# All convolution gates ahead of the mamba gates, and layer norm, output projection and group norm among the last SSD group's steps

## The chip, the cores and the metric

The kernel runs on one core of a Trainium2 chip. The metric is the device time of one execution in microseconds (us). Engines are called as the profile calls them: PE (TensorE's matmuls), PEld (its weight loads), DVE (VectorE), ACT (ScalarE), POOL (GpSimd) and SP (the queue that issues most DMAs).

## The reference, cut to what matters

One layer of a hybrid decoder on 336 tokens (272 of a prompt with meta tokens, 8 sequences of 8 new ones). One input projection feeds a convolution branch (GLU, a depthwise convolution of width 31, layer norm, SiLU, output projection) and a Mamba-2 branch (short convolution, SSD, gated group norm, output projection). Two gates weigh the branches; a product-key expert mixer follows.

```python
proj = xn @ w_in + b_in
glu_in, z, xbc, dt_raw, gate_raw = split(proj)
ga, gb = split(glu_in)
u = ga * sigmoid(gb)
c = causal_depthwise(concat(conf_buf, u), conf_dw_w, conf_dw_b)
c = silu(layernorm(c, conf_ln_g, conf_ln_b))
y_a = c @ w_conf_out + b_conf_out
...
ys, h = ssd_segment(xs, dt, A, Bm, Cm, h, chunk)
y = gated_group_rmsnorm(ys + D_skip * xs, z, m_norm_w)
y_b = y @ w_m_out
g_a, g_b = split(sigmoid(gate_raw))
x = x + (g_a * y_a + g_b * y_b) @ w_o
x = x + peer(rmsnorm(x, norm2_w), peer_w_q, peer_keys, peer_u, peer_v)
```

## The kernel before

Features lie on the partitions, in tiles of 128 rows and 336 token columns (T); D_MODEL is 8 such tiles (KD). A projection to 128 features (`proj`) is 24 matmuls: for each of the eight input tiles the weight's high part times the input's high and low parts, then eight with the weight's low part. `weight` loads 128x1024 weights with a DMA on the SP queue into one of four `wraw` buffers, casts the high part `wh` on ACT and subtracts the low part `wl` on POOL, or now and then on DVE (the share `lm`); there are two `wh` and two `wl` buffers. `split` makes the same two parts of an input. PSUM has three banks for projections (`pj`), two for small products (`misc`) and two for the SSD's outputs (tag `y`).

The mixer's first part is a loop over 8 groups (G). In turn g, the generator `ssd` of group g gives its PE steps between the projections of group g+1 (`conf`, `xbc`, `zproj`), and the last steps of group g-1 (`old`) come in between too: `run(old, 1)` and `run(new, 1)` let one step of each go after each projection. The last step of a group squares its output on ACT, adds the two halves on POOL (tile `sq`) and sums groups on PE (`pgn`, line 641), then on DVE. In the last turn there is no next group: the projections of the gates (`gate`, 16 in all, `gates`) take that place, with the layer norm of the convolution branch written among them: `norm_mean` (PE sums `csum` and the last `cbuf` tile; ACT scales the mean; DVE subtracts it from eight `cbuf` tiles; ACT squares them into `sq`, of which there are four buffers), `norm_var` (PE sums eight squares), `norm_scale` (DVE scales `cbuf`, ACT applies SiLU).

After the groups: `gnorm_stats` (DVE and ACT make the group norm's factors from `pgn` into the tile `acs3`, which the profile calls acs), `gnorm` of each group (PE spreads the factors into `pgb`, DVE multiplies), `gsplit` (the parts `yh` on ACT and `yl` on POOL and DVE). `conf_out(j)` is the convolution branch's output projection of 128 features, from `ch` and `cl`, the two parts of `cbuf`, weighed with the gate. Then for each j the two projections of `w_mo` and the gated sum, its parts `mh` and `ml`, and the projections of `w_o`, `w_q` and the expert part.

The order: a scheduler orders each engine's instructions by the written order and its own estimates. From the SSD's first group on, and until `pin[0] = False`, PE's matmuls stand exactly in written order (`tc.keep_in_program_order` in `mm`). ACT's functions that need a table are chained in written order (`chain`). All engines execute in order.

Of the kernel before, what the change touches and what calls it, by code (L numbers as in the profile page):

```python
# [7 lines left out]
F32 = mybir.dt.float32  # L8
F32R = mybir.dt.float32r
# [4 lines left out]
OP = mybir.AluOpType  # L14
# [34 lines left out]
LM = (0.05, 0.05, 0.1, 0.5)  # L49
CE = 1  # L50
LOW = 400
NCO = 3
NW0 = 3
RB = 4
OH = 2
UV = 5
GLAG = 14
PLACE = (38, 50)
NB = 7
NG = 10  # L60
LASTP = 122
RIGHT = "right"
TOPK = 16
# [72 lines left out]
def body(tc, ia, oa, stop=None):  # L136
    nc = tc.nc
    with ExitStack() as top:
# [522 lines left out]

        def gsplit(g):
            yh = pair(F32R, "yh")
            yl = m2.tile([128, 2, T], F32R, name="yl", bufs=7) if g else pair(F32R, "yl")
            for b in range(2):
                split(yh[:, b, :], yl[:, b, :], ygf[g][:, b, :], on_pool=b == 0)
            yg.append((yh, yl))

        def gate_tile(j):
            if j < 6 or j > 11:  # L670
                return mp.tile([128, T], F32, name="gs", bufs=6)
            if j < 8:
                return tp.tile([128, T], F32, name="xnf", bufs=2)
            if j < 10:
                return tp.tile([128, MCAT], F32, name="mcat", bufs=2)[:, :T]
            if j == 10:
                idle.append(tp.tile([128, 2, T], F32, name="sz", bufs=2))
            return idle[0][:, j - 10]

        idle = []  # L680

        def gate(j):
            w = weight(ia["w_in"], 64 + j)
            p = pj()
            proj(p, w, xn)
            s = gate_tile(j)
            nc.scalar.activation(s, p, AF.Identity, bias=V("b_in", 64 + j))
            gates.append(s)

        gates, pv, squares, r24 = [], [], [], []  # L690

        def norm_mean():
            pm = pj()
# [4 lines left out]
            for k in range(KD):  # L698
                nc.vector.tensor_tensor(cb[:, k, :], cb[:, k, :], mu, op=OP.subtract)
                sq = tp.tile([128, T], F32, name="sq", bufs=4)  # L700
                nc.scalar.activation(sq, cb[:, k, :], AF.Square)
                squares.append(sq)

        def norm_var(ks):
            if not pv:
                pv.append(pj())
            for k in ks:
                mm(pv[0], ones, squares[k], start=(k == 0), stop=(k == KD - 1))

        def norm_scale():  # L710
            rs = tp.tile([128, T], F32, name="rs", bufs=2)
            rstd_of(rs, pv[0], D, tp)
            for k in range(KD):
                nc.vector.tensor_tensor(cb[:, k, :], cb[:, k, :], rs, op=OP.mult)
                act(cb[:, k, :], cb[:, k, :], AF.Silu, scale=V("ln_g", k), bias=V("ln_b", k))

        pgn = mp.tile([G, T], F32, name="pgn")
        csum = mp.tile([128, T], F32, name="csum")
# [13 lines left out]
        for g in range(G):  # L732
            new = ssd(g, *tiles, sz)
            if g + 1 < G:
                tiles, steps = xbc(g + 1)
                tasks = conf(g + 1) + steps
            else:
                lm[0] = LM[1]
                tasks = [lambda: gate(len(gates))] * 4
            run(old, 1)  # L740
            run(new, 1)
            for f in tasks:
                f()
                run(old, 1)
                run(new, 1)
            if g + 1 < G:
                sz, zsteps = zproj(g + 1)
                zsteps[0]()
# [1 line left out]
                zsteps[1]()  # L750
                old = new
            else:
                norm_mean()
                gate(4)
                run(new, 1)
                norm_var(range(4))
                run(new, 1)
                gate(5)
                run(new, 1)
                norm_var(range(4, KD))  # L760
                norm_scale()
                gate(6)
                run(new, 3)
        nc.scalar.dma_start(oa["mconv"], mnew)
        ls.close()

        m2 = mix.enter_context(tc.tile_pool(name="m2", bufs=1))
        r24.append(gnorm_stats())
        while len(gates) < NB:
            gate(len(gates))  # L770
        for g in range(G):
            gnorm(g, r24[0])
            if g % 3 == 1 and len(gates) < NG:
                gate(len(gates))
        pin[0] = False
        lm[0] = LM[2]
        ch = m2.tile([128, KD, T], F32R, name="ch")
        cl = m2.tile([128, KD, T], F32R, name="cl")
        for k in range(KD):
            split(ch[:, k, :], cl[:, k, :], cb[:, k, :])  # L780

        def conf_out(j):
            ga = gates[2 * j]
            act(ga, ga, AF.Sigmoid)
            w = weight(ia["w_co"], j)
            p = pj()
            proj(p, w, rows(ch, cl))
            nc.vector.scalar_tensor_tensor(ga, p, V("b_co", j), ga, op0=OP.add, op1=OP.mult)

        for j in range(NCO):  # L790
            conf_out(j)
        for g in range(G):
            gsplit(g)
        mh = m2.tile([128, KD, T], F32R, name="mh")
        ml = m2.tile([128, KD, T], F32R, name="ml")

        for j in range(KD):
            while len(gates) < min(2 * j + 3 + NG - 2 * NCO, 16):
                gate(len(gates))
            if j >= NCO:  # L800
                conf_out(j)
            ga, gb = gates[2 * j:2 * j + 2]
            act(gb, gb, AF.Sigmoid)
            p = pj()
            for s in range(2):
# [595 lines left out]
```

## Time and profile before

| what | us |
| --- | --- |
| median of 3 runs | 1430.98 (1429.24 to 1433.15) |
| the profiled execution's own time | 1431.76 |
| its span in the profile | 1430.0 |
| PE busy in the span | 1334.6 (93%) |
| DVE busy | 1007.1 (70%) |
| ACT busy | 525.8 (37%) |
| POOL busy | 582.3 (41%) |

The page also cuts the span into 40 slices of 35.75 us; a digit is the busy share of a slice in tenths, for PEclk the granted clock of TensorE:

```profile
PE   5899999999986999999999889999979999988997
PEclk9899999999987999999999999999989999999999
DMA  5444543544421444444999899999999999999993
```

The 12th and 13th slice (393 to 465 us) are the end of the SSD: PE 8 and 6 tenths, its clock 8 and 7 there. From the 20th slice on the expert part streams its tables, with DMA at 9 tenths. In the timelines a row is start, us, engine, line, operation, output<-inputs, shapes, count, and in brackets the engine's idle time ahead of it with what ended it. Rows of a group or a tile show the count, then ns of one: least, median, most.

### The profile page before, as it was taken

The numbers are of one execution on the slowest core, as the hardware profiler recorded it, in microseconds if no ns is written. First come the engines' busy times: TensorE is split into PE (matmuls) and PEld (weight loads), VectorE is DVE, ScalarE is ACT, GpSimd is POOL, SyncE is SP. The second block draws the span as 40 slices with busy tenths as digits, with TensorE's granted clock in tenths as the row PEclk, the third lists the DMA queues.
The fourth block names the chain that finished last, engine by engine and source line by source line (L and its number), as shares of the span: only waits on it lengthen the run. The fifth ranks groups of instructions, "written<-read, shape, count | busy, mean of one in ns | idle before, by whom it ended". The sixth has DMA issues, their size and how long they took to land.

```text
span 1430.0 us, 24506 instructions
## 1 busy us (share of the span) xinstructions
PE 1334.6 (93%) x9308; PEld 1261.6 (88%) x9308; DVE 1007.1 (70%) x2326; ACT 525.8 (37%) x1347; POOL 582.3 (41%) x483
## 2 busy tenths in 40 slices
PE   5899999999986999999999889999979999988997
PEld 3898888888865999989899889999979999987997
DVE  6787778777656312669999976787788787776423
ACT  4587776777646343443222221111111100111001
POOL 2267667767653666754221242222232222242100
PEclk9899999999987999999999999999989999999999
DMA  5444543544421444444999899999999999999993
GB/s 183 151 130 155 172 149 119 170 155 152 150 78 63 143 145 138 150 163 135 391 416 412 331 412 414 406 373 392 384 417 415 394 379 384 385 417 415 414 335 98
DMA packets 86806, 382.05 MB, mean 267 GB/s; under 512 B 10112, under 2 KB 15360, under 8 KB 66080
## 3 DMA queue, kind: packets, MB, share of 16 engines
q1 hardware_dynamic: 64144, 226.87, 44.1%
q0 software_dynamic: 20736, 151.00, 26.0%
q10 hardware_dynamic: 1808, 2.60, 0.5%
q8 instruction: 73, 1.20, 0.3%
q14 instruction: 45, 0.37, 0.1%
HBM read 367.41 MB, written 13.03 MB: 266 GB/s over the span
## 4 chain that ended last, share of the span: by engine, by line
PE 51%; DVE 13%; DMA 6%; ACT 1%; POOL 0%; issue 0%; DVEq 0%; ACTq 0%
PE va L1267 19%; PE pj L150 14%; PE pj L1176 12%; PE pg L1205 5%; DMA eraw<-in_vE_dram 3%; DVE ygat L1110 2%; DVE wuv L1102 2%; DMA eraw<-in_uT_dram 2%; DVE si L912 1%; DVE cand L955 1%; DMA nd<-x1d 1%; PE psc L1012 1%; DVE si L909 1%; DVE cand L949 1%; DVE cand L952 1%; DVE ci L909 0%
## 5 line engine op out<-in xcount | busy, mean ns | idle before, releaser
L990 POOL DMA_INDIRECT wuv<-in_peer_uv_dram,gid x144 | 179.7, 1248 | 511.2 <-DVE ygat L1110 218.5
L215 POOL TENSOR_TENSOR wl<-wraw,wh 128x1024 fp32r<-128x1024 f32 x115 | 274.9, 2390 | 190.1 <-ACT wh L214 107.3
L1176 PE MATMUL pj<-nd,eraw 128*128 128x176 f32 x2048 | 324.7, 318 | 10.5 <-DMA eraw<-in_uT_dram 7.2
L1267 PE MATMUL va<-S,eraw 128*128 128x176 f32 x2048 | 315.2, 314 | 11.0 <-DMA eraw<-in_vE_dram 11.0
L1176 PEld LDWEIGHTS pj<-nd,eraw 128*128 128x128 f32 x2048 | 311.5, 193 | 13.8 <-ACT S L1178 8.5
L1267 PEld LDWEIGHTS va<-S,eraw 128*128 128x128 f32 x2048 | 306.1, 191 | 15.7 <-DMA eraw<-in_vE_dram 13.9
L150 PE MATMUL pj<-ah,wh 128*128 128x336 f32 (+1 forms) x768 | 250.0, 334 | 2.4 <-ACT xnf L195 2.1
L150 PE MATMUL pj<-al,wh 128*128 128x336 f32 (+1 forms) x768 | 241.3, 322 | 0.0
L1110 DVE SCALAR_TENSOR_TENSOR ygat<-wuv,scg,ygat 128x1024 f32<-128x1024 f32 x128 | 163.9, 1280 | 53.4 <-ACT scg L1105 53.2
L214 ACT CAST wh<-wraw 128x1024 fp32r<-128x1024 f32 x128 | 134.4, 1050 | 148.9 <-PE pj L150 79.4
L1102 DVE SCALAR_TENSOR_TENSOR wuv<-wuv,x2m 128x1024 f32<-128x1024 f32 x128 | 155.9, 1218 | 38.2 <-DMA wuv<-in_peer_uv_dram,gid 38.2
L1104 ACT ACTIVATE scg<-scg 128x1 f32<-128x1 f32 x144 | 29.0, 202 | 401.9 <-DVE wuv L1102 401.7
L393 DVE SCALAR_TENSOR_TENSOR pcv<-ccat,vec,pcv 128x272 f32<-128x272 f32 x464 | 151.7, 388 | 17.9 <-ACT pcv L391 17.9
L150 PEld LDWEIGHTS pj<-ah,wh 128*128 128x128 f32 x768 | 148.5, 194 | 12.2 <-issue 4.4
L150 PEld LDWEIGHTS pj<-al,wh 128*128 128x128 f32 x768 | 148.7, 194 | 1.1 <-DVE al L215 0.5
L150 PE MATMUL pj<-ah,wl 128*128 128x336 f32 (+1 forms) x768 | 138.7, 320 | 0.0
L150 PEld LDWEIGHTS pj<-ah,wl 128*128 128x128 f32 x768 | 123.1, 190 | 0.8 <-issue 0.7
L1178 ACT ACTIVATE S<-pj 128x176 f32<-128x176 f32 x128 | 37.7, 311 | 155.4 <-PE pj L1176 155.3
L1205 PE MATMUL pg<-oh 128*128 128x64 bf16 x1056 | 76.3, 241 | 0.0
L1205 PEld LDWEIGHTS <-oh 128*128 128x128 bf16 x1056 | 71.6, 117 | 2.4
L1212 DVE TENSOR_TENSOR S<-S,pg 128x192 f32<-128x192 f32 (+1 forms) x66 | 31.7, 508 | 50.5 <-PE pg L1205 50.4
L408 DVE SCALAR_TENSOR_TENSOR pj<-mcat,vec,pj 128x360 f32<-128x360 f32 x96 | 56.4, 587 | 0.5 <-ACT pj L406 0.3
(343 smaller groups left out, 1691.5 us busy)
## 6 DMA issues: line engine op xcount, KB each, us to landing
eraw<-in_uT_dram SPq DMA_DIRECT2D x128, 512.0 KB, 11.5
eraw<-in_vE_dram SPq DMA_DIRECT2D x128, 512.0 KB, 10.0
wraw<-in_w_in_dram SPq DMA_DIRECT2D x80, 512.0 KB, 3.6
st<-in_state_dram SPq DMA_DIRECT2D x8, 1024.0 KB, 5.2
out_ssm_s_dram<-st SPq DMA_DIRECT2D x8, 1024.0 KB, 4.8
wraw<-in_w_mo_dram SPq DMA_DIRECT2D x16, 512.0 KB, 3.5
wraw<-in_w_q_dram SPq DMA_DIRECT2D x16, 512.0 KB, 3.6
wraw<-in_w_co_dram SPq DMA_DIRECT2D x8, 512.0 KB, 3.5
```

The source lines that it names most:

```text
L150: i_ = nc.tensor.matmul(*a_, **kw)
L214: (nc.vector.tensor_copy if on_dve else nc.scalar.copy)(h, src)
L215: (nc.gpsimd if on_pool else nc.vector).tensor_tensor(l, src, h.bitcast(F32), op=OP.subtract)
L393: t = nc.vector.scalar_tensor_tensor(o, i_, wv, a_, op0=OP.mult, op1=OP.add)
L408: nc.vector.scalar_tensor_tensor(o, cat[:, w:w + n], wv, o, op0=OP.mult, op1=OP.add)
L990: i_ = nc.gpsimd.indirect_dma_start(out=u, out_offset=None, in_=ia["peer_uv"], in_offset=bass.IndirectOffsetOnAxis(ap=gid[:, c:c + 1], axi ...
L1102: nc.vector.scalar_tensor_tensor(u[:, :D], u[:, :D], 1.0, x2m if c < NPICK else x2e, op0=OP.mult, op1=OP.mult, accum_out=w)
L1110: nc.vector.scalar_tensor_tensor(a_, u[:, D:], scg[:, c:c + 1], a_, op0=OP.mult, op1=OP.add)
L1176: i_ = nc.tensor.matmul(p[:, :ND], raw[:, k, :], nd[:, k, :], start=(k == 0), stop=(k == KD - 1))
L1178: nc.scalar.activation(Sv(b), p[:, :ND], AF.Gelu)
L1205: i_ = nc.tensor.matmul(pg[:, q, :], B[:, q // 4, :, q % 4], A[:, c_, q // 4, :, q % 4], start=(c_ == 0), stop=(c_ == 2))
L1267: i_ = nc.tensor.matmul(va[k // 2][:, k % 2], raw[:, k, :], Sv(b), start=False, stop=(b == 127), skip_group_check=True)
```

## The change

The gates are made in another order: all eight of the convolution branch (`j` even) first, then the eight of the mamba branch; in the list `gates` the first eight are the convolution's. The last turn of the group loop has seven gates as its tasks instead of four. `norm_mean` is written behind the first of them instead of behind the fourth, and adds its squares on POOL, so that `norm_scale`, which takes over the variance's matmul, needs one product instead of eight; it is written behind the fourth gate and makes `ch` and `cl` as well. The last three steps of the SSD have `conf_out` 0 to 2 between them, `gnorm_stats` is followed by a gate and `conf_out` 3 and 4, and `gnorm`, `gsplit` and `conf_out` 5 to 7 are written in one loop. Three gates follow; the last five stand one each ahead of the `w_mo` projections. `cl` takes idle tiles of other names (ccat, sz, mcat), some gates have new tiles (ge, gx).

```diff
...
@@ -661,33 +658,46 @@
 
         def gsplit(g):
             yh = pair(F32R, "yh")
-            yl = m2.tile([128, 2, T], F32R, name="yl", bufs=7) if g else pair(F32R, "yl")
+            yl = m2.tile([128, 2, T], F32R, name="yl", bufs=8)
             for b in range(2):
                 split(yh[:, b, :], yl[:, b, :], ygf[g][:, b, :], on_pool=b == 0)
             yg.append((yh, yl))
 
...
         idle = []
 
-        def gate(j):
+        def gate():
+            n = len(gates)
+            j = 2 * n if n < KD else 2 * (n - KD) + 1
             w = weight(ia["w_in"], 64 + j)
             p = pj()
             proj(p, w, xn)
-            s = gate_tile(j)
+            s = gate_tile(n)
             nc.scalar.activation(s, p, AF.Identity, bias=V("b_in", 64 + j))
             gates.append(s)
 
-        gates, pv, squares, r24 = [], [], [], []
+        ch = mp.tile([128, KD, T], F32R, name="ch")
+        cl = []
+
+        def conf_out(j):
+            ga = gates[j]
+            act(ga, ga, AF.Sigmoid)
+            w = weight(ia["w_co"], j)
+            p = pj()
+            proj(p, w, lambda k: (ch[:, k, :], cl[k]))
+            nc.vector.scalar_tensor_tensor(ga, p, V("b_co", j), ga, op0=OP.add, op1=OP.mult)
+
+        gates, squares, r24 = [], [], []
 
         def norm_mean():
             pm = pj()
@@ -699,20 +709,28 @@
                 nc.vector.tensor_tensor(cb[:, k, :], cb[:, k, :], mu, op=OP.subtract)
                 sq = tp.tile([128, T], F32, name="sq", bufs=4)
                 nc.scalar.activation(sq, cb[:, k, :], AF.Square)
-                squares.append(sq)
-
-        def norm_var(ks):
-            if not pv:
-                pv.append(pj())
-            for k in ks:
-                mm(pv[0], ones, squares[k], start=(k == 0), stop=(k == KD - 1))
+                if k:
+                    nc.gpsimd.tensor_tensor(squares[0], squares[0], sq, op=OP.add)
+                else:
+                    squares.append(sq)
 
         def norm_scale():
             rs = tp.tile([128, T], F32, name="rs", bufs=2)
-            rstd_of(rs, pv[0], D, tp)
+            p = pj()
+            mm(p, ones, squares[0], start=True, stop=True)
+            rstd_of(rs, p, D, tp)
             for k in range(KD):
                 nc.vector.tensor_tensor(cb[:, k, :], cb[:, k, :], rs, op=OP.mult)
                 act(cb[:, k, :], cb[:, k, :], AF.Silu, scale=V("ln_g", k), bias=V("ln_b", k))
+            for k in range(KD):
+                if k in (0, 1):
+                    cl.append(tp.tile([128, CCAT], F32R, name="ccat", bufs=2)[:, :T])
+                elif k in (2, 4):
+                    t = tp.tile([128, 2, T], F32R, name="sz", bufs=2) if k == 2 else pair(F32R, "cl")
+                    cl.extend(t[:, c_, :] for c_ in range(2))
+                elif k > 5:
+                    cl.append(tp.tile([128, MCAT], F32R, name="mcat", bufs=2)[:, :T])
+                split(ch[:, k, :], cl[k], cb[:, k, :])
 
         pgn = mp.tile([G, T], F32, name="pgn")
         csum = mp.tile([128, T], F32, name="csum")
@@ -736,13 +754,18 @@
                 tasks = conf(g + 1) + steps
             else:
                 lm[0] = LM[1]
-                tasks = [lambda: gate(len(gates))] * 4
+                tasks = [gate] * 7
             run(old, 1)
             run(new, 1)
-            for f in tasks:
+            for n, f in enumerate(tasks):
                 f()
                 run(old, 1)
                 run(new, 1)
+                if g + 1 == G:
+                    if n == 0:
+                        norm_mean()
+                    elif n == 3:
+                        norm_scale()
             if g + 1 < G:
                 sz, zsteps = zproj(g + 1)
                 zsteps[0]()
@@ -750,56 +773,33 @@
                 zsteps[1]()
                 old = new
             else:
-                norm_mean()
-                gate(4)
-                run(new, 1)
-                norm_var(range(4))
-                run(new, 1)
-                gate(5)
-                run(new, 1)
-                norm_var(range(4, KD))
-                norm_scale()
-                gate(6)
-                run(new, 3)
+                for j in range(3):
+                    conf_out(j)
+                    run(new, 1)
         nc.scalar.dma_start(oa["mconv"], mnew)
         ls.close()
 
         m2 = mix.enter_context(tc.tile_pool(name="m2", bufs=1))
         r24.append(gnorm_stats())
-        while len(gates) < NB:
-            gate(len(gates))
+        gate()
+        conf_out(3)
+        conf_out(4)
         for g in range(G):
             gnorm(g, r24[0])
-            if g % 3 == 1 and len(gates) < NG:
-                gate(len(gates))
+            gsplit(g)
+            if g % 2 and g < 6:
+                conf_out(5 + g // 2)
+        for _ in range(3):
+            gate()
         pin[0] = False
         lm[0] = LM[2]
-        ch = m2.tile([128, KD, T], F32R, name="ch")
-        cl = m2.tile([128, KD, T], F32R, name="cl")
-        for k in range(KD):
-            split(ch[:, k, :], cl[:, k, :], cb[:, k, :])
-
-        def conf_out(j):
-            ga = gates[2 * j]
-            act(ga, ga, AF.Sigmoid)
-            w = weight(ia["w_co"], j)
-            p = pj()
-            proj(p, w, rows(ch, cl))
-            nc.vector.scalar_tensor_tensor(ga, p, V("b_co", j), ga, op0=OP.add, op1=OP.mult)
-
-        for j in range(NCO):
-            conf_out(j)
-        for g in range(G):
-            gsplit(g)
         mh = m2.tile([128, KD, T], F32R, name="mh")
         ml = m2.tile([128, KD, T], F32R, name="ml")
 
         for j in range(KD):
-            while len(gates) < min(2 * j + 3 + NG - 2 * NCO, 16):
-                gate(len(gates))
-            if j >= NCO:
-                conf_out(j)
-            ga, gb = gates[2 * j:2 * j + 2]
+            if len(gates) < 2 * KD:
+                gate()
+            ga, gb = gates[j], gates[KD + j]
             act(gb, gb, AF.Sigmoid)
             p = pj()
             for s in range(2):
```

The constants NCO, NB and NG go; the rest of the cut is `gate_tile`, which picks a gate's tile. Line numbers of the changed kernel are 3 lower in the code ahead of line 660 (L215 becomes L212, L638 becomes L635).

The first place is POOL in the last group's first steps. `sq<-sq` of L638 adds the two halves of group 6's squares for `pgn`; `wx` are products of the last group. Before:

```order
L585 TENSOR_TENSOR xg<-xg,sz 128x336
L215 TENSOR_TENSOR wl<-wraw,wh 128x1024
L638 TENSOR_TENSOR sq<-sq 128x336
L215 TENSOR_TENSOR wl<-wraw,wh 128x1024
L533 TENSOR_TENSOR wx_4561<-xt_4558,wd_202 80x256
L215 TENSOR_TENSOR wl<-wraw,wh 128x1024
L533 TENSOR_TENSOR wx_4623<-xt_4620,wd_226 128x256
L533 TENSOR_TENSOR wx_4632<-xt_4629,wd_242 128x256
```

Now, with the layer norm's seven additions as L713:

```order
L582 TENSOR_TENSOR xg<-xg,sz 128x336
L212 TENSOR_TENSOR wl<-wraw,wh 128x1024 x2
L530 TENSOR_TENSOR wx_4562<-xt_4559,wd_202 80x256
L212 TENSOR_TENSOR wl<-wraw,wh 128x1024
L713 TENSOR_TENSOR sq<-sq 128x336 x7
L635 TENSOR_TENSOR sq<-sq 128x336
L530 TENSOR_TENSOR wx_4660<-xt_4657,wd_226 128x256
L530 TENSOR_TENSOR wx_4669<-xt_4666,wd_242 128x256
```

Group 6's addition moved behind two weight splits, the first `wx` and the seven new additions; the other two `wx` stand behind it as before.

The second place is PE at the first `pgb`, the spreading of the group norm's factors; `pj<-ah` is a gate's projection, `pst` the last state update, `pgn` the last group's sum. Before:

```order
L150 MATMUL pst_4960<-wx_4561,Bm 128x256
L150 MATMUL pst_4961<-wx_4561,Bm 128x256
L150 MATMUL pgn<-sq,cstm 8x336
L150 LDWEIGHTS id_256
L150 MATMUL pgb<-acs_4992,id_256 128x336
L150 LDWEIGHTS id_256
L150 MATMUL pgb<-acs_4992,id_256 128x336
L150 MATMUL pj<-ah,wh 128x336
```

Now, where `pj<-ch` is a projection of `conf_out` (the one ahead of these rows is `conf_out` 3; this is the end of `conf_out` 4):

```order
L147 MATMUL pj<-ch,wh 128x336
L147 MATMUL pj<-mcat,wh 128x336
L147 MATMUL pj<-ch,wl 128x336 x8
L147 LDWEIGHTS id_256
L147 MATMUL pgb<-acs_5114,id_256 128x336
L147 LDWEIGHTS id_256
L147 MATMUL pgb<-acs_5114,id_256 128x336
L147 MATMUL pj<-ch,wh 128x336
```

`pgn` no longer stands right ahead of the first `pgb`: a gate and `conf_out` 3 and 4, 72 matmuls, stand between them.

More of the change, by code (lines that the diff above doesn't have):

```diff
@@ L51 @@
 LOW = 400
-NCO = 3
 NW0 = 3
@@ L58 @@
 PLACE = (38, 50)
-NB = 7
-NG = 10
 LASTP = 122
@@ L667, in gsplit, with gate_tile @@
             yg.append((yh, yl))
-        def gate_tile(j):
-            if j < 6 or j > 11:
+        def gate_tile(n):
+            if n < 3 or 7 <= n < 10:
                 return mp.tile([128, T], F32, name="gs", bufs=6)
-            if j < 8:
+            if n < 5:
+                return mp.tile([128, T], F32, name="ge", bufs=2)
+            if n < 7:
                 return tp.tile([128, T], F32, name="xnf", bufs=2)
-            if j < 10:
-                return tp.tile([128, MCAT], F32, name="mcat", bufs=2)[:, :T]
-            if j == 10:
+            if n == 10:
                 idle.append(tp.tile([128, 2, T], F32, name="sz", bufs=2))
-            return idle[0][:, j - 10]
+            return idle[0][:, n - 10] if n < 12 else m2.tile([128, T], F32, name="gx", bufs=4)
         idle = []
-        def gate(j):
+        def gate():
+            n = len(gates)
+            j = 2 * n if n < KD else 2 * (n - KD) + 1
             w = weight(ia["w_in"], 64 + j)
```

## The prediction

> **What bounds the kernel now.** I read three views of the profile in this order: the busy time by stage, the waits of TensorE (PE), and the timelines of the engines in the stage that the change rewrites. The page's span, and the stages (start and end in us, length; busy us and instructions of PE, weight load, VectorE, ScalarE, GpSimd; PE's granted clock; DMA share; GB/s):
>
> ```profile
> span 1430.0 us, 24506 instructions
> 300.00:380.00 80.00, 78.34 (x549) 69.66 (x550) 66.18 (x182) 57.23 (x138) 57.49 (x57) 1.00 0.45 150
> 396.50:460.80 64.30, 42.92 (x233) 36.16 (x233) 41.34 (x74) 35.61 (x67) 26.32 (x22) 0.79 0.20 65
> 460.80:580.00 119.20, 119.20 (x777) 119.20 (x776) 35.69 (x44) 48.10 (x63) 69.65 (x31) 1.00 0.43 139
> ```
>
> PE is the bound: before 380 it is 98% busy, after 460.8 it has no gap. Between lie 64.3 us in which it idles 21.4 us and is granted 0.79 of its clock. That is the end of the SSD, and the change reorders just this. The rest of the program keeps its order, so what is won or lost here moves all that follows by as much. PE's waits in this stage (line, releaser, total us, times, longest):
>
> ```profile
> PE pgb L150 <- DVE acs L225: 12.0, 1, 12.0
> PE pst L150 <- DVE st L595: 5.0, 1, 5.0
> PE pst L150 <- DVE dec L543: 2.1, 1, 2.1
> PE pgb L150 <- DVE xg L660: 2.0, 2, 1.1
> PE pgn L150 <- DVE st L595: 0.3, 1, 0.3
> ```
>
> Together 21.4 us. PE runs its instructions in the order written here, so each wait stops all behind it. PE's timeline (start, us; in brackets the idle time before):
>
> ```profile
> 380.59 0.43 PE L150 MATMUL pj<-ah,wh 128*128 128x336 f32 x1
> 384.51 0.73 PE L150 MATMUL pgn<-sq,cstm 128*8 128x336 f32 x2
> 386.71 0.42 PE L150 MATMUL pj<-ah,wh 128*128 128x336 f32 x1
> 396.52 0.83 PE L150 MATMUL pj<-csum,cst 128*128 128x336 f32 x2
> 397.50 0.57 PE L150 MATMUL pj<-ah,wh 128*128 128x336 f32 x1
> 402.13 2.42 PE L150 MATMUL pj<-sq,cst 128*128 128x336 f32 x8
> 406.65 0.70 PE L150 MATMUL pst<-wx,xt 128*128 128x256 f32 x2 [2.10 <-DVE dec L543]
> 409.41 0.63 PE L150 MATMUL pj<-ah,wh 128*128 128x336 f32 x1
> 430.77 1.28 PE L150 MATMUL pgn<-sq,cstm 128*8 128x336 f32 x2 [0.28 <-DVE st L595]
> 444.01 0.72 PE L150 MATMUL pgb<-acs,id 96*128 96x336 bf16 x2 [11.96 <-DVE acs L225]
> 444.31 0.69 PE L150 MATMUL pj<-ah,wh 128*128 128x336 f32 x1
> 444.81 0.48 PE L150 MATMUL pj<-al,wh 128*128 128x336 f32 x1
> 450.17 0.46 PE L150 MATMUL pgb<-acs,id 96*128 96x336 bf16 x2
> 457.30 124.32 PE pj L150 x808
> ```
>
> The last row, of the chain of waits, gives the full pace: 124.32/808 = 0.154 us a matmul, 3.69 us for a projection of 24. The projection after the longest wait took 450.17 - 444.31 = 5.86 us: **a wait costs itself and a slow restart of about 2.2 us** (matmuls of 0.48 us).
>
> **The change, part by part.** Counts first: 16 gates, 8 projections of conf_out, 32 weight splits and their DMAs stay; they change places. PE does one matmul of the squares (2 rows) in place of eight (16 rows). GpSimd (POOL) gets seven additions.
>
> *Work removed.* Four squares took 2.42 us, eight 4.84, one keeps 0.6: **4.2 us** less on PE, all in this stage.
>
> *The 12.0 us.* From the last pgn to the first pgb passed 444.01 - 430.77 = 13.2 us, with no PE work between. Now gate 7, conf_out 3 and 4 stand there: 3 x 3.69, with pgn's 0.7 = 11.8. The chain loses the cl subtractions among its VectorE steps and gains one weight split ahead of it and one weight cast on ScalarE between its table loads; I take it as it was: a remainder of 1.4, less the 0.8 by which pgn (1.28 for 0.73) and pgb (0.72 for 0.46) were themselves slow then: **0.6** left, bounds 0 and 3.
>
> *The 5.0, 0.3 and 2.0 us.* The state update waited for VectorE, which was in the middle of eight scalings of cbuf. Now conf_out 1 (3.69) stands between the two updates, and the scalings are over by then. Between the pairs of pgb there are projections of 3.69 for VectorE's four products. I take 0 for all three.
>
> *A new wait at pgn of group 6.* This is the price. The mean and squares move to just after gate 0, and on ScalarE and POOL the square sum of group 6 now stands behind them, while on PE its matmul (pgn) still follows gate 1. Behind pgn queue the transposes and everything of the last group.
>
> ```profile
> 382.93 0.41 ACT L622 ACTIVATE Bm<-xt,cstm 64x128 f32<-64x128 f32 x1
> 383.43 1.05 ACT L214 CAST wh<-wraw 128x1024 fp32r<-128x1024 f32 x1
> 397.96 0.45 ACT L697 ACTIVATE rs<-pj 128x336 f32<-128x336 f32 x1 [1.63 <-PE pj L150]
> 400.52 0.48 ACT L701 ACTIVATE sq<-cbuf 128x336 f32<-128x336 f32 x1 [2.11 <-DVE cbuf L699]
> 384.72 2.36 POOL L215 TENSOR_TENSOR wl<-wraw,wh 128x1024 fp32r<-128x1024 f32 x1 [2.99 <-ACT wh L214]
> 419.11 0.92 POOL L638 TENSOR_TENSOR sq<-sq 128x336 f32<-128x336 f32 x1 [0.60 <-ACT sq L637]
> L699 DVE TENSOR_TENSOR cbuf<-cbuf,rs x8: 497/498/2651, 398.4 to 403.3; 128x336 f32<-128x336 f32 x8
> ```
>
> PE: mean matmuls 380.6 to 381.6 (396.52 to 397.50 before: 0.98), gate 1 to 385.3. ScalarE is free at 383.3 (after Bm): mean 383.8; first subtraction on VectorE, first square by 385.2; then the weight cast, 386.3. POOL's weight split, ahead of the additions, runs 386.4 to 388.8. Then seven additions and group 6's own, 8 x 0.92 = 7.4, and 0.3 of handoffs: 396.5. Squares and subtractions come faster than 0.92 each and hide under the additions; three of the four sq buffers rotate, each free again after an addition, so they follow at its pace. pgn at 396.6 instead of 385.3: **11.3 us** of new wait. Below: no handoffs, 10.9. Above: each of the eight subtractions (0.50) holds an addition off, 15.3.
>
> *The wait of pst for dec.* The third dec product stood behind the eight subtractions (2.1 us of wait); now it stands behind the eight scalings.
>
> ```profile
> 401.47 0.38 PE L150 MATMUL pcb<-bc 128*128 128x128 f32 x2
> 405.92 0.68 DVE L543 TENSOR_TENSOR dec<-dec,pcb 128x512 f32<-128x512 f32 x1
> 418.16 0.51 DVE L204 TENSOR_SCALAR rsv<-pj 128x336 f32<-128x336 f32 x1 [1.83 <-PE pj L150]
> 421.59 5.59 DVE L714 TENSOR_TENSOR cbuf<-cbuf,rs 128x336 f32<-128x336 f32 x8
> 421.90 2.40 POOL L215 TENSOR_TENSOR wl<-wraw,wh 128x1024 fp32r<-128x1024 f32 x1 [1.88 <-ACT wh L214]
> ```
>
> From pgn to gate 2 took 2.2 us, now 3.5 with the slow restart: gate 2 at 400.1. From there to pgn's old successor, the mean (386.71 to 396.52), 9.8, with a rest of the restart 10.3: the variance matmul at 410.4, done 411.0. VectorE: from rsv to the first scaling 3.4, the scalings 5.6, dec 0.7: 420.9. PE: gate 4, pcb and pst (401.47 to 402.13: 0.7), gate 5: 411.0 + 3.69 + 0.7 + 3.69 = 419.1. A wait of 1.8; bounds 0 and 4.1 (a second scaling held off for 2.2). I take the **2.1** that stood there, the nearest row.
>
> *Clock.* Restarts after a wait of 2 us or more: three before, two now. **2.2 us** less.
>
> *Conf_out 0 to 2, where the output projection enters the last steps.* Each needs its weight cast on ScalarE, and ch and cl. ScalarE's rows:
>
> ```profile
> 424.70 4.01 ACT L195 ACTIVATE cbuf<-cbuf,vec 128x336 f32<-128x336 f32 x7 [0.38 <-DVE cbuf L714]
> 433.01 1.28 ACT L195 ACT_TABLE_LOAD   x1 [4.30 <-DVE rsv L204]
> 437.89 2.35 ACT L195 ACTIVATE gs<-gs 128x336 f32<-128x336 f32 x6
> 440.52 3.06 ACT L214 CAST ch<-cbuf 128x336 fp32r<-128x336 f32 x8
> ```
>
> From the first scaling (414.6 by the count above, 415.1 done) ScalarE has eight SiLUs (4.6), eight ch casts (3.1), two table loads (2.6), two weight casts (2.1), three sigmoids (1.2) and an eviction (0.5): 429.2. PE, after the wait for dec (421.2): pst, py and po 2.8 (406.65 to 409.41 before), gate 6 with what the restart still costs, some 1.0 of 2.2, 4.7, the second py and po about half of the 2.8, 1.4: conf_out 0 at 430.1. So ch is there a microsecond early. I take 0; bounds 0 and 2. On the SP queue the state's write-out (it waits for the second update) now stands ahead of the last conf_out weight; six projections, 22 us, lie between that update and this weight's use. I take 0. Later gates now stand between the w_mo projections where gates and conf_out stood before; the stage's row has ScalarE busy 48 and POOL 70 of 119 us, so 0.
>
> **Sum.** 21.4 + 4.2 + 2.2 - 11.3 - 2.1 - 0.6 = 13.8 us less. The profiled execution took 1431.76 (span 1430.0 and 1.76 around it), 0.8 above the median 1430.98. 1431.76 - 13.8 = 1418.0.
>
> And it does reach the end: the last 730 us keep their DMAs and PE work, and their first DMA waits for buffers that the stage before sets free, so they start 13.8 us earlier.
>
> ```profile
> 700.00:1430.00 730.00, 687.69 (x5100) 675.95 (x5099) 537.20 (x1035) 119.14 (x440) 175.56 (x139) 0.98 0.96 380
> ```
>
> Here DMA is busy 0.96 of the time: nothing is won in it, but nothing is given back either.
>
> **Rivals.** What a measurement can tell from no change is 0.3%, 4.3 us.
>
> *VectorE and POOL hold each other off.* L699's row has 2651 ns beside 498; and L714's eight scalings, with a weight split of POOL beside them (421.90), took 5.59 us, where eight of 0.50 take 4.0. Now eight subtractions meet eight additions, and eight scalings meet a split. Price: 4.0 us at pgn and 2.2 at dec, 6.2 together: 7.6 us less, 1424. For it speak these rows; against it, that POOL's additions need not lose the turn.
> The Trainium skill, "SBUF — State Buffer", section "Who interferes with whom", says that a VectorE instruction with two inputs in SBUF contends with a GpSimd instruction that reads SBUF, and that whoever issues first holds the port pair for the whole instruction. The 2651 ns agree; by this rule alone the time would be this rival's.
>
> *ScalarE becomes the bound of the conf_out projections (slower).* Eight SiLUs (4.6), eight ch casts (3.1), eight weight casts (8.4), five table loads (6.4) and eight sigmoids (3.1) now crowd between 414 and 456. A weight cast that comes late makes its projection start late, eight times over: at x us each the sum is 13.8 - 8x. From x = 1.2 the change can't be told from none, from x = 2.3 it is slower; at 2.5 it takes 1438. For it: 25.6 us of work in 42, in an order that also waits for PE. Against it: each weight cast is written one projection, 3.69 us, ahead of its use.
>
> *The new wait is short.* If POOL's split came after the additions, pgn would wait 2.4 less, and with no wait at dec, 4.5 more is won: 1413 to 1414. The order of POOL speaks against it.
>
> **Chances.** Forecast (10 to 18 us less) 0.58; holding off (4.3 to 10 less) 0.22; short wait 0.04; ScalarE within 0.3% 0.09, slower 0.07. Faster 0.84, same 0.09, slower 0.07. With the unknown costs all low the sum is 16.9 (1414, from the median), so 1413 below; the holding-off case ends at 1427 above. 1413 to 1427 keep 0.84.
>
> **What would show it.** Right: PE waits 10 to 15 us for POOL's sq at pgn after gate 1, about 2 us for dec at pst, and no long wait at pgb; squares on PE two rows. Wrong: a wait at pgb of more than 3 us (the chain outlasted its cover), PE waiting for ScalarE's wh or ch at conf_out (the second rival), subtractions of more than 1 us beside POOL's additions (the first).

## The result, and the profile after

| | median | range | runs |
| --- | --- | --- | --- |
| before | 1432.07 us | 1429.24 to 1434.11 | 4 |
| after | 1417.99 us | 1416.2 to 1419.32 | 4 |

The ratio is 0.9902, with a 95% interval of 0.9887 to 0.9918: 14.1 us less, by the interval 12 to 16. The profiled execution after took 1419.32 us, 12.4 less than the one before.

The page's strips of after, 35.4 us a slice now: the dent lies in the 11th and 12th slice (354 to 425 us), with 8 and 7 tenths of PE at a clock of 9 and 7; in the 12th and 13th slice before it was 8 and 6 at a clock of 8 and 7.

```profile
PE   5899999999879999999999889999979999987997
PEclk9899999999979999999999999999989999999999
```

PE's waits in the stage, read as before (line, releaser, total us, times, longest). The first is new. The second, for dec, stands where 2.1 us stood before, but now behind the scalings instead of the subtractions. Of the other four waits only pgb's is left, 1.6 us of 12.0. No wait stands at a conf_out.

```profile
PE pgn L147 <- POOL sq L635: 10.8, 1, 10.8
PE pst L147 <- DVE dec L540: 2.7, 1, 2.7
PE pgb L147 <- DVE acs L222: 1.6, 1, 1.6
```

PE's timeline of after, from the mean, which opens the stage now, to the first w_o projection:

```profile
379.10 0.72 PE L147 MATMUL pj<-csum,cst 128*128 128x336 f32 x2
394.88 1.29 PE L147 MATMUL pgn<-sq,cstm 128*8 128x336 f32 x2 [10.78 <-POOL sq L635]
408.53 0.83 PE L147 MATMUL pj<-sq,cst 128*128 128x336 f32 x2
420.09 1.22 PE L147 MATMUL pst<-wx,xt 128*128 128x256 f32 x2 [2.67 <-DVE dec L540]
430.40 0.40 PE L147 MATMUL pj<-ch,wh 128*128 128x336 f32 x1
457.71 0.44 PE L147 MATMUL pgb<-acs,id 96*128 96x336 bf16 x2 [1.55 <-DVE acs L222]
558.56 0.32 PE L147 MATMUL pj<-mh,wh 128*128 128x336 f32 x1
```

Before, the stage opened with gate 1 at 380.59, and the first w_o matmul stood here:

```profile
571.60 0.31 PE L150 MATMUL pj<-mh,wh 128*128 128x336 f32 x1
```

So the stage with the gates behind it took 191.0 us before and 179.5 after: **11.5 us** are the change's own. Another 1.5 us of this execution's lead was there before the stage began (379.10 for 380.59), where the two programs are the same; in the kernels below, whose code ahead of the stage is the same, such differences come and go as well.

What stands behind the 10.8 us, on POOL and ScalarE (start, us, engine, line, ..., count, idle time and its end):

```profile
384.24 2.66 POOL L212 TENSOR_TENSOR wl<-wraw,wh 128x1024 fp32r<-128x1024 f32 x1 [4.11 <-ACT wh L211]
386.86 7.12 POOL L713 TENSOR_TENSOR sq<-sq 128x336 f32<-128x336 f32 x7
393.93 0.89 POOL L635 TENSOR_TENSOR sq<-sq 128x336 f32<-128x336 f32 x1
```

```profile
385.14 0.47 ACT L711 ACTIVATE sq<-cbuf 128x336 f32<-128x336 f32 x1
388.04 0.48 ACT L711 ACTIVATE sq<-cbuf 128x336 f32<-128x336 f32 x1 [2.43 <-POOL sq L713]
393.04 0.48 ACT L634 ACTIVATE sq<-xg 128x336 f32<-128x336 f32 x1 [0.49 <-POOL sq L713]
```

The split, seven additions, then group 6's: POOL works from 384.2 to 394.8 without a gap. ScalarE has four squares done at 385.6 and then gets a buffer per addition; the two squares of group 6 (L634) come last.

### The profile page after: what moved, and what is told of

Same layout as the page of the kernel before. It is cut to its first block, busy times and chain, and to the rows that moved or that the text cites. A ratio compares the mean times of both kernels' runs of the same rounds, so it can differ in the third digit from the quotient of the medians.

```text
span 1417.5 us, 24480 instructions
## 1 busy us (share of the span) xinstructions
PE 1328.0 (94%) x9294; PEld 1255.3 (89%) x9294; DVE 1013.6 (72%) x2326; ACT 526.4 (37%) x1348; POOL 589.0 (42%) x490
## 4 chain that ended last, share of the span: by engine, by line
PE 76%; DVE 13%; DMA 7%; ACT 2%; issue 1%; POOL 1%; DVEq 0%; SPq 0%; POOLq 0%; ACTq 0%
PE pj L147 31%; PE va L1267 19%; PE pj L1176 12%; PE pg L1205 4%; DMA eraw<-in_vE_dram 3%; PE pst L147 2%; DVE ygat L1110 2%; DMA eraw<-in_uT_dram 2%; DVE wuv L1102 2%; PE po L147 1%; PE pdec L147 1%; PE py L147 1%; DMA nd<-x1d 1%; PE ptr L152 1%; DVE si L912 1%
## 5 line engine op out<-in xcount | busy, mean ns | idle before, releaser
L990 POOL DMA_INDIRECT wuv<-in_peer_uv_dram,gid x144 | 176.8, 1228 | 515.8 <-DVE ygat L1110 220.2
L212 POOL TENSOR_TENSOR wl<-wraw,wh 128x1024 fp32r<-128x1024 f32 x115 | 276.3, 2404 | 187.5 <-ACT wh L211 114.3
L1267 PE MATMUL va<-S,eraw 128*128 128x176 f32 x2048 | 315.8, 314 | 11.5 <-DMA eraw<-in_vE_dram 11.5
```

Source lines behind the costliest of these rows:

```text
L212: (nc.gpsimd if on_pool else nc.vector).tensor_tensor(l, src, h.bitcast(F32), op=OP.subtract)
L990: i_ = nc.gpsimd.indirect_dma_start(out=u, out_offset=None, in_=ia["peer_uv"], in_offset=bass.IndirectOffsetOnAxis(ap=gid[:, c:c + 1], axi ...
L1267: i_ = nc.tensor.matmul(va[k // 2][:, k % 2], raw[:, k, :], Sv(b), start=False, stop=(b == 127), skip_group_check=True)
```

## The experiments

All are edits of the changed kernel unless said otherwise. The last column is the start of the first w_o matmul in the profiled execution; the stretch ahead of the stage, the same in all of them, makes it differ by up to about 2 us. What follows that matmul took 858 to 865 us in the profiled executions (858.4 before, 858.9 in the changed kernel, 865.4 in less_cover), so a median also carries differences that don't come from the stage.

| kernel | median us | ratio to before, 95% | PE's waits of 1 us and more in the stage | w_o |
| --- | --- | --- | --- | --- |
| changed kernel | 1417.99 | 0.9887 to 0.9918 | pgn 10.8, dec 2.7, pgb 1.6 | 558.6 |
| adds_vector | 1418.29 | 0.9866 to 0.9932 | pgn 8.6, dec 2.7, pgb 1.6 | 555.2 |
| squares_early | 1423.20 | 0.9919 to 0.9975 | variance 6.8, transposes 3.6, conf_out 2.0, pgb 1.6 | 562.7 |
| adds_vector_squares_early | 1411.46 | 0.9829 to 0.9883 | transposes 2.9, dec 3.2, pgb 1.5 | 550.2 |
| sums_on_pe | 1414.92 | 0.9863 to 0.9913 | transposes 2.9, dec 1.5, pgb 1.6 | 551.8 |
| mean_later_pool | 1417.67 | 0.9890 to 0.9952 | variance 10.2, conf_out 1.4, pgb 1.6 | 555.9 |
| mean_later_vector | 1406.28 | 0.9797 to 0.9841 | variance 2.9, pgb 1.5 | 545.7 |
| pgn_early | 1408.74 | 0.9816 to 0.9859 | dec 4.4, pgb 1.5 | 547.7 |
| pgn_early_all | 1406.52 | 0.9803 to 0.9842 | dec 2.7 | 544.1 |
| all_edits | 1407.95 | 0.9801 to 0.9849 | variance 2.9 | 544.8 |
| less_cover | 1427.11 | 0.9954 to 0.9985 | pgn 10.8, pgb 6.4, dec 2.7 | 565.8 |
| no_vector_split | 1418.25 | 0.9861 to 0.9918 | pgn 10.8, dec 2.7 | 557.9 |
| outputs_behind | 1424.03 | 0.9914 to 0.9962 | pgn 11.2 and 2.8, dec 2.7, update 1.5 | 560.7 |

### What makes the new wait at pgn: the order, or POOL's time?

**adds_vector**, the additions on the other engine:

```diff
-                    nc.gpsimd.tensor_tensor(squares[0], squares[0], sq, op=OP.add)
+                    nc.vector.tensor_tensor(squares[0], squares[0], sq, op=OP.add)
```

> The seven additions of squares go from POOL to VectorE; the order stays, so group 6's squares still stand behind the layer norm's. If the new wait at pgn (10.8 us) is POOL's row of additions (7.12 us), it shrinks: VectorE takes about 0.5 us for each, the last rotating buffer comes free about 388.5, group 6's addition ends about 390.5 instead of 394.8: a wait of 6 to 7 us, 1413 to 1414 us. If only the order makes the wait, it stays at 10 us and the time at 1418. If the end of the program hangs on something else than PE's waits here, the time stays too, with a shorter wait.

The wait was 8.6 us: less than with POOL's additions, more than the 6 to 7 forecast. VectorE's timeline shows why: the subtractions, with a POOL split beside them (2.66 us from 383.79), took 5.58 us instead of 4.0, the additions 4.17 instead of 3.5.

```profile
381.64 5.58 DVE L709 TENSOR_TENSOR cbuf<-cbuf,rs 128x336 f32<-128x336 f32 x8 [2.66 <-ACT rs L707]
387.15 4.17 DVE L713 TENSOR_TENSOR sq<-sq 128x336 f32<-128x336 f32 x7
```

The median did not move (runs from 1413 to 1420): in the profiled execution the first w_o matmul came 3.3 us earlier, but what follows it took 3.8 us longer. Another engine alone doesn't remove the wait, since group 6's squares still stand behind.

**squares_early**, the order alone: in `ssd`, for group 6, the squares and their addition stand one step earlier.

```diff
-            yield
+            if g != G - 2:
+                yield
             sq = [tp.tile([128, T], F32, name="sq", bufs=4) for _ in range(2)]
...
+            if g == G - 2:
+                yield
             p = misc([G, T], "pgn")
```

> Only group 6's two squares and their addition are written one step earlier, ahead of the layer norm's mean; pgn stays behind gate 1, and POOL keeps the seven additions. Both theories: the wait at pgn is gone. If that wait was only the order (a finished sum held behind others), 10.8 us and about 1.2 of a slow restart come back: 1406. If POOL hasn't the time for the seven additions among its splits, they now end after the variance matmul is due (POOL's row from 384: three splits of 2.4, seven additions of 0.95, eight st scalings 4.6, two wx 1.2, one hs 0.9 = 20.6, to about 404, against 395 on PE): a wait of 8 to 9 us moves to the variance matmul, and the time is 1415 to 1417.

The wait at pgn was gone, and the time was longer than the changed kernel's, 1423.2, and longer than either theory had it (1406, or 1415 to 1417): PE now waited for the additions at the variance's matmul.

```profile
PE pj L147 <- POOL sq L716: 6.8, 1, 6.8
PE ptr L152 <- DVE pgn L644: 3.6, 1, 3.6
PE pj L147 <- DVE mcat L212: 2.0, 1, 2.0
```

POOL's timeline of this kernel has the additions (L716) between splits and scalings to 407.9; the matmul was due at 401.1:

```profile
403.12 2.35 POOL L212 TENSOR_TENSOR wl<-wraw,wh 128x1024 fp32r<-128x1024 f32 x1
405.99 1.87 POOL L716 TENSOR_TENSOR sq<-sq 128x336 f32<-128x336 f32 x2
```

The theory "only the order" falls here. The 3.6 us were in neither theory: pgn's addition on VectorE stands behind the eight subtractions, and the transposes behind pgn wait for its PSUM bank.

```profile
381.24 6.29 DVE L712 TENSOR_TENSOR cbuf<-cbuf,rs 128x336 f32<-128x336 f32 x8 [2.66 <-ACT rs L710]
387.45 0.48 DVE L644 TENSOR_TENSOR pgn<-pgn 8x336 f32<-8x336 f32 x1
```

The waits together are no longer than in the changed kernel (14.9 us for 15.1). What makes this kernel the slower one, by 5 us in the stage, is the clock: its trace has three slow stretches, 5.6 us at a granted clock of 0.52, 6.2 at 0.52 and 9.1 at 0.51. Times the missing share of the clock that is 10.1 us, against 5.4 in the changed kernel.

**adds_vector_squares_early**, both edits:

> Both: group 6's squares one step earlier, and the seven additions on VectorE. The wait at pgn is gone and the variance matmul, due about 395, finds its sum ready (VectorE: 4.0 of subtractions from 382, 3.5 of additions). 10.8 us and about 1.2 of a slow restart: 1406 us, if what PE waits for here reaches the end in full. If ScalarE or the output projection's inputs have no slack (the second rival), the gain comes back as a wait at the first conf_out and the time stays above 1412.

1411.5 us: a gain of 6.5 on the changed kernel where 12 were forecast. Neither pgn nor the variance waits, but the transposes (2.9) and dec (3.2, for 2.7) take part of it back:

```profile
PE pst L147 <- DVE dec L540: 3.2, 1, 3.2
PE ptr L152 <- DVE pgn L644: 2.9, 1, 2.9
```

**sums_on_pe**: group 6's squares early, no additions; PE sums eight squares with `norm_var` of before, four behind gate 2 and four behind gate 3.

> Group 6's squares one step earlier, and the variance summed on PE from eight squares as before the change (four rows behind gate 2, four behind gate 3), with no additions at all. No wait at pgn. Against the kernel with both edits it costs PE 16 rows of 0.30 us for two: 4.2 us more, about 1410, if PE is the bound throughout; about 1406, the same as that one, if a wait for VectorE or ScalarE (dec, the scalings) hides the matmuls.

1414.9, against 1411.5 with VectorE's additions: 3.5 more, where 4.2 were forecast, though the intervals of the two ratios overlap. In the profiled executions the first w_o matmul is only 1.7 us later; the wait for dec is 1.5 instead of 3.2. So part of what the matmuls cost seems to be hidden by that wait, as the second half of the expectation had it.

### The place of the mean

**mean_later_pool** and **mean_later_vector**: the mean is written behind the second gate's steps, behind pgn; in the second kernel the additions are on VectorE as well.

```diff
-                    if n == 0:
+                    if n == 1:
                         norm_mean()
```

> The changed kernel with nothing but the mean behind the second gate's steps; the seven additions stay on POOL. If the place of the mean is all that costs here, the time is the 1406 us of the kernel that has the additions on VectorE too. If POOL has no time for them, they end about 404 (as in the kernel with early squares, where the variance matmul waited 6.8 us), the variance matmul, due at 395, waits 7 to 9 us, its successors wait 2 to 3 us at the first conf_out, and the time is 1413 to 1416.

> The changed kernel with the layer norm's mean written behind the second gate's steps (so behind pgn of group 6) instead of behind the first, and the seven additions on VectorE. In the kernel with early squares a wait of 2.9 us was left because pgn's addition on VectorE stands behind the eight subtractions and the transposes wait for its bank. Here it stands ahead of them: no wait at pgn, none at the transposes, and the sum of squares is ready by about 394 to 395 for a variance matmul due at 396. 1411.5 - 2.9 = about 1408 us. If the norm is now too late instead (mean at 385, not 379), the wait goes to the variance matmul or to the first conf_out, and the time stays at 1411 to 1414.

With the additions on POOL the wait only moved: 10.2 us (7 to 9 expected) at the variance's matmul, and the time is the changed kernel's (1417.67 for 1417.99).

```profile
PE pj L147 <- POOL sq L713: 10.2, 1, 10.2
```

With the additions on VectorE 2.9 us are left of it, and the time is 1406.28 (1405.32 to 1406.47), 11.7 below the changed kernel and with no overlap. The last addition ends at 397.9, not at 395:

```profile
390.93 5.55 DVE L713 TENSOR_TENSOR sq<-sq 128x336 f32<-128x336 f32 x5
```

five additions at 1.1 us each, where 0.5 had been forecast; one of them took 2.2 us, beside a weight split of POOL. The two kernels differ in the engine of seven additions alone: by the medians that is worth 11.4 us with the mean at this place, and nothing in the changed kernel's order (1418.29). By the first w_o matmul the engine alone brings 3.3 us, the place alone 2.7, and both together 12.8. It takes both.

### Further gains

**pgn_early** lets the step with pgn go behind gate 0, ahead of the mean (the `yield` ahead of it is left out for group 6); **pgn_early_all** and **all_edits** also write the scalings one gate later (`norm_apply`, the second half of `norm_scale`) and set VectorE's share of the weight splits to 0.

```diff
-                        norm_scale()
+                        rs = norm_scale()
+                    elif n == 4:
+                        norm_apply(rs)
```

> Group 6's squares and pgn stand behind gate 0, ahead of the mean, and the additions are on VectorE: a gate more lies between the mean and the variance matmul than with the mean behind the second gate. There the variance matmul waited 2.9 us and ran at half pace for 8 us behind it; here it should not wait, which is worth 2.9 and some 3 of slow pace. But then PE is at the third dec product early, and the wait of 2.7 to 3.2 us for dec comes back with a slow stretch of 4 to 6.6 us (2 to 3 us lost). So 1404 to 1408, about the same: one wait exchanged for the other. If dec doesn't wait either, 1400 to 1402.

> As the one before, with the scalings written behind the fifth gate's steps (the third dec product then stands behind four of the eight) and no weight split on VectorE. No wait of over 1 us is left up to the end of the group norm, if ScalarE keeps up with the first conf_out: 1400 to 1403 us. If the later scalings make ch late, the first conf_outs wait 1 to 3 us, and the time is 1403 to 1407, no better than the kernel with the mean behind the second gate.

> The mean behind the second gate, the additions on VectorE, the eight scalings and SiLUs written behind the fifth gate's steps instead of behind the fourth (so that the third dec product need not wait for all eight), and no weight split on VectorE. If each wait is worth what it shows: 1408 as with the first two edits, less 2.7 to 3.2 at dec and up to 1.2 at pgb: about 1404 us. If the later scalings eat the slack of ScalarE (ch is ready 2.4 us ahead of the first conf_out in the changed kernel), a wait of 1 to 2 us appears there and the time is 1405 to 1408.

All three end with mean_later_vector, between 1406.5 and 1408.7. pgn_early exchanged the variance's wait for one at dec, as expected, but of 4.4 us. pgn_early_all missed its 1400 to 1403: the third dec product stands behind four scalings instead of eight, and PE still waits 2.7 us for it. One instruction ahead of the scalings took 2.58 us, and the four scalings 4.24 where 2.0 would be four of 0.50:

```profile
400.03 2.58 DVE L208 SCALAR_TENSOR_TENSOR rs<-rsv,rst 128x336 f32<-128x336 f32 x1
402.64 4.24 DVE L727 TENSOR_TENSOR cbuf<-cbuf,rs 128x336 f32<-128x336 f32 x4
```

In all_edits dec and pgb have no wait, but the variance's 2.9 us are as in mean_later_vector, and no time is won that could be measured. The best kernel is thus the two-line edit, mean_later_vector.

### The cover, the weight split, and conf_out between the steps

**less_cover** takes `conf_out(3)` and `conf_out(4)` from between `gnorm_stats` and the loop of `gnorm`, and writes them behind that loop.

> The changed kernel with conf_out 3 and 4 taken from between the last pgn and the first pgb and written behind the group norm's loop. If these projections only covered the chain of the group norm's factors, the wait at pgb grows from 1.6 by up to 2 x 3.69 to 9.0 us, with a slow restart of 1 to 2 us behind it: 1426 to 1428 us. If the chain itself gets shorter because two weight casts on ScalarE (1.05 each) and two evictions on VectorE (0.57) have left it, the wait is 6 to 7 us: 1423 to 1425. If something else removed the 12 us, the time stays at 1418.

The time went up 9.1 us, to 1427.1. The wait at pgb grew by 4.8, to 6.4: the chain did get shorter, with its last cast done at 455.0 instead of 457.7. Most of these 2.7 us are not the casts and evictions that the expectation named: with no split of POOL beside it, the chain's own last cast took 0.33 us instead of 2.39. Behind the wait came a slow restart, 6.9 us at a clock of 0.60: 4.8 + 6.9 x 0.40 = 7.6, and the first w_o matmul is 7.3 later.

```profile
PE pgb L147 <- DVE acs L222: 6.4, 1, 6.4
```

**no_vector_split** sets the second number of `LM` from 0.05 to 0.0.

> The changed kernel with no weight split on VectorE in this stage (one stood ahead of the last addition to pgn, 1.22 us; POOL takes it). If this split makes the 1.6 us of wait at pgb, the wait falls to about 0.4 and the time by 1.2, to 1417 us, which only the trace can show. If the cast of acs (2.39 us for 0.33) that stands beside POOL's splits makes it, the wait stays at 1 to 2 us.

The wait at pgb is gone altogether. The row is from the view of the tile acs (count, ns of one: least, median, most, first and last start). Not only the split ahead of pgn's addition went (1.22 us); with POOL's splits at other times the last cast took 0.33 us again. The time can't show it: 1418.25.

```profile
L222 DVE CAST acs<-s3r x1: 325/325/325, 452.9 to 452.9; 8x336 bf16<-8x336 f32 x1
```

**outputs_behind** writes `conf_out` 0 to 2 behind the SSD's last three steps (`run(new, 3)` ahead of them).

> The changed kernel with conf_out 0 to 2 taken from between the SSD's last three steps and written behind them. If the 5.0 us of wait for the state update came from the scalings alone, which are now long over on VectorE (419 against 431), no such wait returns: at most 1 us at the second update (two additions of 0.64), but about 2.7 us at the last pgn, whose squares are not ready yet (yo at 431.9, then POOL 0.9 and 0.9, ScalarE 0.5, POOL 0.9: about 435.7, against 433 on PE), with a slow restart of 2; the 1.6 us at pgb goes, since three more projections cover it: 1419 to 1422 us. If conf_out 1 between the updates was needed, a wait of 3 to 5 us stands at the second update and the time is above 1423.

The update waited 1.5 us and the last pgn 2.8. The 5.0 us of before don't come back: that the scalings are earlier removes most of that wait by itself, and the projections between the updates the rest. The time is 6 us above the changed kernel's. Up to the first w_o matmul, 2.1 us later, the trace accounts for nearly all of it: 3.1 us more of waits, less 1.3 at the half clock, since no slow stretch followed the wait for dec here (see the last section). The profiled execution needed another 2.0 us behind that matmul; why stays open.

## Why the prediction was right, and where only its total was

Point by point, as the prediction put it.

- **"The 12.0 us" and the cover.** Right. Gate 7 and conf_out 3 and 4 cover the chain; without the last two the wait is 6.4. The rest was 1.6 for 0.6 forecast, inside its bounds. What was missed is the last cast of the chain, which took 2.39 us beside POOL's splits (0.33 before); the weight split ahead of the chain, 1.22, had been named:

```profile
444.76 1.22 DVE L212 TENSOR_TENSOR wl<-wraw,wh 128x1024 fp32r<-128x1024 f32 x1
455.26 2.39 DVE L222 CAST acs<-s3r 8x336 bf16<-8x336 f32 x1
```

- **"The 5.0, 0.3 and 2.0 us": 0.** Right; none is left.
- **"A new wait at pgn of group 6": 11.3.** Right in place and size, 10.8. The links of the sum hold too: POOL's split began when forecast (384.2, which with this execution's lead of 1.5 us is 385.7 for 386.4), the additions came back to back, and ScalarE waited for rotating buffers. That split and the eight additions then took 10.6 us where 10.1 had been counted, so the early start and the longer work nearly cancel. But its reason was told as a matter of order, and by the experiments that is half of it: POOL has no time for seven additions in this stretch. In the two other orders tried they hold PE up at the variance's matmul instead, 6.8 us or 10.2.
- **"The wait of pst for dec": 2.1.** It was 2.7, inside 0 to 4.1; but it had been counted out as 1.8 from steps of which two are off, in opposite directions. An instruction ahead of the scalings took 2.58 us, with POOL's split beside it (0.51 before), so that from rsv to the first scaling passed 6.5 us and not 3.4. The eight scalings, no longer beside a split, took 3.4 us and not the 5.6 counted:

```profile
413.39 2.58 DVE L208 SCALAR_TENSOR_TENSOR rs<-rsv,rst 128x336 f32<-128x336 f32 x1
416.00 3.44 DVE L723 TENSOR_TENSOR cbuf<-cbuf,rs 128x336 f32<-128x336 f32 x8
```

- **The squares on PE: 4.2.** By the rows right: two rows of matmuls instead of sixteen. sums_on_pe shows the same work at 3.5 us of time, and 1.7 at the first w_o matmul, probably in part hidden by dec.
- **"Restarts after a wait of 2 us or more: three before, two now. 2.2 us less."** This term was mis-sized. The restarts have no fixed price. What the half clock cost is the length of a slow stretch times the missing share of the clock. Before, by stage (start and end, length, ..., the third number from the end the granted clock):

```profile
427.80:432.05 4.25, 3.95 (x10) 1.94 (x11) 1.85 (x3) 0.91 (x2) 0.00 (x0) 0.50 0.00 0
444.00:451.60 7.60, 6.62 (x28) 6.12 (x28) 5.67 (x12) 4.04 (x8) 2.94 (x3) 0.68 0.01 2
406.70:411.30 4.60, 4.60 (x27) 4.00 (x28) 1.72 (x4) 0.00 (x0) 1.51 (x2) 0.63 0.41 140
```

  These are 4.25 x 0.50 + 7.60 x 0.32 + 4.60 x 0.37 = 6.3 us; after, 4.3 and 6.5 us at 0.50 (rows in the last section), 5.4: 0.9 less, not 2.2.
- **"It does reach the end".** Right: the first w_o matmul came 13.0 us earlier, the span is 12.5 shorter.
- **ScalarE at conf_out 0: "ch is there a microsecond early".** Right that there is no wait. But conf_out 0 started at 430.40, which with the lead of 1.5 us is 431.9 for 430.1 forecast: the half clock behind dec cost more than the part of a restart that was counted. The margin is thin: where the norm ends later, PE waits 2.0 us in squares_early and 1.4 in mean_later_pool, and both times for a cl part from VectorE, not for ScalarE.

So the sum should have been 21.4 - 15.1 + 4.2 + 0.9 = 11.4, and the stage shows 11.5. PE's busy time in the stage says the same of the last two terms: 169.5 us before and 164.5 after, 5.1 less. The forecast's 13.8 agrees with the difference of the medians, 14.1, partly by luck: 1.1 of waits and 1.3 of clock were missed, and as much lies in the differences between executions.

The rivals. *Holding off* happened, but not where it was priced. Each time a VectorE instruction took about as long as a POOL weight split beside it: 2.58 and 2.39 us in the rows above, and 2.65 for one of the eight subtractions, beside the split that ran from 384.24 to 386.90. That subtraction was the seventh. When POOL came to its additions only the eighth was left (1.19 us, beside the first addition, 1.15), so the two rows of eight hardly met, and the 4.0 us at pgn were not paid:

```profile
382.09 6.28 DVE L709 TENSOR_TENSOR cbuf<-cbuf,rs 128x336 f32<-128x336 f32 x8 [2.66 <-ACT rs L707]
```

*ScalarE as the bound* and *the short wait* did not come.

## What to carry to other kernels

A wait that an edit creates on the path is not removed by moving what waits: first count whether the engine that makes it late has the time at all between the first and the last use; here the same seven additions made PE wait 10.8, 6.8 and 10.2 us in the three orders with them on POOL, and 2.9 once both their engine and their place were changed. Where instructions of the bound engine are pinned in written order, write the finished work of an older group ahead of a new chain, including its small steps on other engines (pgn's addition), since each can hold a buffer that someone behind it needs. And price a wait with the slow pace behind it, as a range: here it added 1.6 to 4.4 us to the waits of 2 us and more, and nothing to one of 2.69.

## What the runs showed of the hardware that was not expected

**The slow pace behind a wait doesn't follow the wait's length.** Stretches of after, in the view of busy time by stage (the third number from the end is PE's granted clock): behind 10.78 us of wait, behind 2.67, and behind the 1.55 at pgb.

```profile
394.90:399.20 4.30, 4.30 (x15) 2.18 (x16) 1.54 (x4) 1.60 (x5) 1.23 (x2) 0.50 0.00 0
420.10:426.60 6.50, 6.50 (x30) 5.52 (x31) 3.43 (x8) 6.47 (x13) 5.55 (x4) 0.50 0.19 47
457.80:461.00 3.20, 3.20 (x22) 3.15 (x22) 3.20 (x6) 1.28 (x3) 2.99 (x2) 1.00 0.64 179
```

The shorter wait had the longer slow stretch, 6.5 us against 4.3. In the other kernels waits of 2.0 to 2.9 us mostly had 3 to 9 us of it behind them (3.1 us at 0.50 behind 2.85 in all_edits, 9.1 at 0.51 behind 2.01 in squares_early), and the 1.5 us at pgb none in any. One of 2.69 us, in outputs_behind, had none either. It stands at dec, with the same work around it as the 2.67 of the changed kernel, and PE went on at a granted clock of 1.00: the two matmuls took 0.70 us, where they took 1.22 there.

```profile
419.96 0.70 PE L147 MATMUL pst<-wx,xt 128*128 128x256 f32 x2 [2.69 <-DVE dec L540]
422.01 0.40 PE L147 MATMUL pj<-ah,wh 128*128 128x336 f32 x1
```

And 1.53 us at dec in sums_on_pe did have one, which began only when PE had already worked for 1.6 us:

```profile
414.60:416.20 1.60, 1.56 (x16) 1.06 (x16) 1.60 (x4) 1.60 (x4) 0.81 (x1) 1.00 0.00 0
416.30:419.70 3.40, 3.40 (x16) 3.40 (x15) 3.40 (x4) 3.37 (x6) 2.30 (x1) 0.50 0.21 49
```

The Trainium skill, "TensorE: Matmul & The Clock Gate", Part 1 on the clock gate, has windows of about 3.4 us that run freely, so that the point of a change depends on where in the window the work falls. That the stretches differ so much, and that one is missing, agrees with it. That the half clock comes after at least one idle window, as the same part has it, does not agree with the waits of 2.67 and 1.53 us here.

**A small cast can be held for 2.4 us.** The chain's last cast, of 8x336, took 2.38 to 2.43 us in the nine kernels in which a weight split of POOL (2.4) had begun ahead of it, and 0.33 in the other five, before among them. In the Trainium skill, "SBUF — State Buffer", section "Who interferes with whom", casts are among the operations that can take the port pair shared with GpSimd for the whole instruction; these rows agree.
